# Key transposes moved, layer norm in pairs by twos, constants' loads spaced, the last two experts by output block

## The chip, the cores and the metric

The kernel runs on one core of a Trainium2 chip. The metric is the device time of one execution in microseconds (us); every time below is in us unless it is marked otherwise. TensorE is called PE, VectorE DVE, ScalarE ACT, GpSimd POOL, and SyncE, which here only issues transfers, SP.

## The reference

Two transformer blocks in a row on a sequence of 256 tokens of width 1024. The first block ends in a layer of product keys over 16384 experts, which is where most of the time goes:

```python
scores = jnp.einsum("bshpd,hpnd->bshpn", q, sub_keys)          # 8 heads, 2 halves, 128 keys
s_top, i_top = lax.top_k(scores, 16)                           # per half
best, pos = lax.top_k(cand, 16)                                # cand: sums of the two halves' best
idx = jnp.take_along_axis(cand_idx, pos, axis=-1)
gates = jax.nn.softmax(best, axis=-1)
act = jax.nn.gelu(einsum("td,ted->te", xt, expert_u[idx]), approximate=False)
y = einsum("te,ted->td", gates * act, expert_v[idx])
...
a, b, g = jnp.split(h @ w_in, 3, axis=-1)                      # second block, layer 0
y = conv(a * jax.nn.sigmoid(b)) + db                           # 31 taps
y = jax.nn.silu(layernorm(y, ln_g, ln_b)) * jax.nn.silu(g)
x = x + gt * (y @ w_out)
...                                                            # layer 1: window means
```

Here `gt` and its companions come from a modulation `silu(c) @ w_mod + b_mod` that does not depend on x.

## The kernel before, in words

**Experts without a gather.** The kernel computes all 16384 experts for all 256 tokens and multiplies by a matrix of gates that is zero where an expert was not chosen. `peer_up` multiplies 128 tiles of `expert_u` (128 experts x 1024 each) with the tokens and applies the gelu, `gates` makes the gates and multiplies them on, `peer_down` multiplies with 128 tiles of `expert_v`. Each is done in two halves of 64 tiles. The transposed sum is held in four PSUM tiles `y`.

**Split precision.** Every weight tile is loaded in f32 (`raw`, on SP's queue, three loads ahead). ACT rounds it to `hi`, a subtraction makes `lo` = raw - hi, and PE does three matmuls for each of the 8 blocks of a tile: `hi` with the high part of x (L153), `hi` with its low part (L154), `lo` with the high part (L155). That is 24 matmuls a tile. `hi` and `lo` have three buffers, so ACT can make `hi` of tile n only when PE is through with tile n-3. The subtraction stands on POOL for three of four tiles in the first half of `peer_up`, and on DVE for every fourth (tiles 3, 7, 11, ...) and for all tiles later on (`split_next`, L142).

**Work beside the matmuls.** DVE finds the best keys while the first 64 tiles run. The generator `side` runs `topk` and then `modulation`; `tick` moves it on by one `yield` after every half tile. `topk` works for two blocks of 128 tokens, tb = 0 and 1. For each it does the two searches (MAX, MAX_INDEX, MATCH_REPLACE), then turns positions into keys with a one-hot product: `oh` is a compare with `iota` (L1154), a product (L1156) and three folding sums (L1159, L1160) that leave `sel`, once for each half of the keys. Three PE transposes `ptk` (L1164 to L1166) bring both halves of `sel` and the gates' numerators `exk` into the layout of `gates`; four DVE copies follow (L1167 to L1170). All of it is put into the engines' queues in the order in which it is emitted, modified by a scheduler; each engine runs its queue in order. `behind` ties each step of `topk` to the last subtraction that stands on DVE.

**Into the second block.** `second_prep`, advanced by the same ticks during the second half of `peer_down`, loads constants (`rcnt`, `fwd`, `ftap`, `dw`, `inv`). After the last expert, h is brought up to date with `y`, the sums of squares s2 (`s` in rows) and `acc` (`ssacc` in rows) are made, and `second` begins, with small matmuls of constants (`wfm`, `wfp`) filling PE.

**The layer norm** lies between the gates of the second block (`gate_evac`, four pairs of weight tiles) and its output product, a `quad` of four tiles that goes through the 8 blocks of x two at a time. With `yc` the centred convolution, `dms` the remaining mean and `rl` the inverse deviation, it makes yc\*rl, subtracts dms\*rl, takes Silu with gain and bias, multiplies with Silu of the gate `sg` and splits the product into `xbh` and `xbl`, which PE needs. This goes on four pairs p of blocks; the subtraction of pairs 1 to 3 stands on POOL.

Of the kernel before, what the change touches and what calls it, by code (L numbers as in the profile page):

```python
# [6 lines left out]
F32 = mybir.dt.float32  # L7
# [7 lines left out]
T = 256  # L15
# [25 lines left out]
class Net:  # L41
# [105 lines left out]
    def block(self, ps, x, first=True):  # L147

        hi, lo = self.take()
        xh, xl = x  # L150
        for k in range(KB):
            w = slice(k * 128, (k + 1) * 128)
            self.P.matmul(ps, lhsT=hi[:, w], rhs=xh[:, k, :], start=(k == 0 and first), stop=False, skip_group_check=True)  # L153
            self.P.matmul(ps, lhsT=hi[:, w], rhs=xl[:, k, :], start=False, stop=False, skip_group_check=True)  # L154
            self.P.matmul(ps, lhsT=lo[:, w], rhs=xh[:, k, :], start=False, stop=(k == KB - 1), skip_group_check=True)  # L155
            if k == KB // 2 - 1:
                self.tick()
# [908 lines left out]
    def topk(self):  # L1066
# [12 lines left out]
        for tb in range(2):  # L1079
# [30 lines left out]
            for h in range(8):  # L1110
                V.max(bv[:, h, 0:8], c[:, h, :])
                V.max_index(bi[:, h, 0:8], bv[:, h, 0:8], c[:, h, :])
                t = top.tile([128, 112], F32, tag="mt", bufs=2, name="ct")
                V.match_replace(t, bv[:, h, 0:8], c[:, h, :], LOW)
                V.max(bv[:, h, 8:16], t)
                V.max_index(bi[:, h, 8:16], bv[:, h, 8:16], t)
                yield
                if h % 2 == 0:
                    yield
# [111 lines left out]
    def peer_down(self, act, half):  # L1231
# [53 lines left out]
    def second_prep(self):  # L1285
# [62 lines left out]
    def second(self):  # L1348
# [7 lines left out]

        acc = self.newacc(post)
        s2 = self.psX.tile([128, 512], F32, tag="x", name="s2")[:, 0:T]
        for p in range(4):
            hp = h[:, 2 * p:2 * p + 2, :]  # L1360
            V.tensor_add(hp, self.y[p], hp)
            sq = post.tile([128, 2, T], F32, tag="ta", bufs=2, name="sq2")
            A.activation(sq, hp, AF.Square)
            for i in range(2):
                k = 2 * p + i
                P.matmul(s2, lhsT=self.gf2[:, k, :], rhs=sq[:, i, :], start=(k == 0), stop=(k == KB - 1))
            if p == 0:
                acc = sq
                sq0 = sq
            elif p == 1:  # L1370
                acc = self.newacc(post)
                V.tensor_add(acc, sq0, sq)
            else:
                V.tensor_add(acc, acc, sq)

# [39 lines left out]
        def b_evac(ps, g):  # L1415
# [74 lines left out]
        def ln_gen(po):  # L1490
# [17 lines left out]
            V.tensor_sub(v, v, dm2)  # L1508
# [17 lines left out]
        xb = self.newx(self.cst, "xb")  # L1526
        first = None
        for p in range(4):
            o, sg = (x[:, 2 * p:2 * p + 2, :] for x in (yc, self.sg))
            with self.tc.issue_after(first.ins) if first else nullcontext():  # L1530
                V.tensor_mul(o, o, self.rowb(self.rl))
            i = (G if p else V).tensor_sub(o, o, self.rowb(self.rlm))
            first = first or i
            with self.tc.issue_after(self.lexp.ins):
                A.activation(sg, sg, AF.Silu)
            for i in range(2):
                k = 2 * p + i
                last = A.activation(o[:, i, :], o[:, i, :], AF.Silu, scale=self.col("ln_g", k), bias=self.col("ln_b", k))
# [231 lines left out]
```

## Time and profile before

| | before |
|---|---|
| median of 3 runs (lowest to highest) | 1368.26 (1366.46 to 1369.71) |
| the profiled run, its own time | 1368.67 |
| span of the profiled run | 1366.6 |
| mean granted clock of PE | 0.979 |
| PE busy | 1297.6 (95%) |
| DVE, ACT, POOL busy | 1016.6 (74%), 643.9 (47%), 188.1 (14%) |
| chain that ended last | PE 83%, DVE 10%, ACT 3%, DMA 2% |

The span runs from the first instruction to the last; 2.07 us of the run lie around it. An engine is busy while it has an instruction in work. The chain is followed back from the last instruction to whatever released each step. The granted clock of PE is a share of full speed: 1.00 is 2.4 GHz, 0.50 is 1.2 GHz. A row such as "PE mm L155 <- DVE lo L142" names the instruction that waited and the one that released it.

### The profile page before, as it was taken

To read this page: it belongs to the slowest core of one execution; us is meant where nothing else is said; L and a number is where in the kernel's file an instruction comes from. 1 tells how busy PE (TensorE), PEld (TensorE's weight loads), DVE (VectorE), ACT (ScalarE), POOL (GpSimd) and SP (SyncE) were. 2 spreads that over 40 slices of the span, in tenths; PEclk is the share of its full clock that TensorE was granted. 3 is DMA by queue.
4 is the path that set the end of the run, shared out by engine and by line. 5 is a ranking of instruction groups with operands and counts; after the bars stand their busy time and mean duration, and the time that the engine had idled before them with its cause. 6 is when DMAs were issued, how large, how long until landed. Compare 5 with 4: busy or idle time off the path is not lost.

```text
span 1366.6 us, 27270 instructions
## 1 busy us (share of the span) xinstructions
PE 1297.6 (95%) x11212; PEld 1268.9 (93%) x11212; DVE 1016.6 (74%) x1879; ACT 643.9 (47%) x843; POOL 188.1 (14%) x182
## 2 busy tenths in 40 slices
PE   7999979999988989999999999998999998996988
PEld 7999969989988989999999999997999996996987
DVE  7897765456789865988887999985666656666884
ACT  6675335546443534344445444444444445355662
POOL 0000000003654654000000000010000000001000
PEclk9999999999999999999999999999999998998999
DMA  7644224344654556766666666666777762442553
GB/s 236 206 139 124 93 78 154 124 154 125 187 168 132 178 164 216 230 208 197 216 206 218 213 204 206 212 213 201 237 235 232 234 197 84 126 130 87 170 165 113
DMA packets 67340, 239.69 MB, mean 175 GB/s; under 512 B 8146, under 2 KB 8402, under 8 KB 67088
## 3 DMA queue, kind: packets, MB, share of 16 engines
q1 hardware_dynamic: 59536, 212.79, 51.0%
q0 software_dynamic: 7680, 25.17, 5.4%
q8 instruction: 87, 1.43, 0.4%
q14 instruction: 37, 0.30, 0.1%
HBM read 236.88 MB, written 1.05 MB: 174 GB/s over the span
## 4 chain that ended last, share of the span: by engine, by line
PE 83%; DVE 10%; ACT 3%; DMA 2%; issue 2%; POOL 1%; SPq 0%; DVEq 0%; ACTq 0%; POOLq 0%
PE mm L155 12%; PE mm L153 12%; PE mm L154 12%; PE y L1255 9%; PE y L1257 9%; PE y L1256 9%; DVE lo L142 2%; PE mmv L209 2%; PE mmv L210 2%; PE mmv L211 2%; PE mm L184 2%; PE mm L185 2%; PE mm L183 2%; ACT hi L140 1%; PE G L1210 1%
## 5 line engine op out<-in xcount | busy, mean ns | idle before, releaser
L140 ACT ACTIVATE hi<-raw 128x1024 fp32r<-128x1024 f32 x391 | 412.8, 1060 | 585.4 <-PE mm L154 234.9
L142 DVE TENSOR_TENSOR lo<-raw,hi 128x1024 fp32r<-128x1024 f32 x343 | 420.2, 1228 | 191.6 <-ACT hi L140 189.0
L155 PE MATMUL mm<-xbh,lo 128*128 128x256 f32 x1128 | 319.9, 284 | 5.8 <-DVE lo L142 5.2
L153 PE MATMUL mm<-xbh,hi 128*128 128x256 f32 x1128 | 322.1, 286 | 0.3 <-ACT hi L140 0.3
L154 PE MATMUL mm<-xbl,hi 128*128 128x256 f32 x1128 | 319.0, 283 | 0.0
L1255 PE MATMUL y<-xbh,hi 128*128 128x256 f32 x1024 | 289.5, 283 | 5.2 <-ACT hi L140 5.2
L1257 PE MATMUL y<-xbh,lo 128*128 128x256 f32 x1024 | 288.6, 282 | 0.5 <-DVE lo L142 0.5
L1256 PE MATMUL y<-xbl,hi 128*128 128x256 f32 x1024 | 288.6, 282 | 0.0
L155 PEld LDWEIGHTS mm<-xbh,lo 128*128 128x128 f32 x1128 | 215.0, 191 | 6.8 <-DVE lo L142 6.2
L153 PEld LDWEIGHTS mm<-xbh,hi 128*128 128x128 f32 x1128 | 215.4, 191 | 0.6 <-ACT hi L140 0.5
L154 PEld LDWEIGHTS mm<-xbl,hi 128*128 128x128 f32 x1128 | 215.6, 191 | 0.0
L1255 PEld LDWEIGHTS y<-xbh,hi 128*128 128x128 f32 x1024 | 194.0, 190 | 5.4 <-ACT hi L140 5.4
L1257 PEld LDWEIGHTS y<-xbh,lo 128*128 128x128 f32 x1024 | 193.6, 189 | 1.5 <-DVE lo L142 0.8
L1256 PEld LDWEIGHTS y<-xbl,hi 128*128 128x128 f32 x1024 | 194.1, 190 | 0.0
L142 POOL TENSOR_TENSOR lo<-raw,hi 128x1024 fp32r<-128x1024 f32 x48 | 120.7, 2521 | 200.1 <-ACT hi L140 198.8
L153 PE MATMUL mm<-xah,hi 128*128 128x256 f32 x448 | 128.6, 288 | 3.2 <-ACT xah L1339 3.2
L154 PE MATMUL mm<-xal,hi 128*128 128x256 f32 x448 | 128.0, 286 | 1.0 <-DVE xal L1340 1.0
L155 PE MATMUL mm<-xah,lo 128*128 128x256 f32 x448 | 128.0, 286 | 0.5 <-DVE lo L142 0.5
L1277 POOL DMA_DIRECT2D wm<-in_w_mod x96 | 51.8, 539 | 519.7 <-DVE wm L1280 500.4
L1280 DVE SCALAR_TENSOR_TENSOR wm<-wm,silu_c 128x512 f32<-128x512 f32 x96 | 70.7, 737 | 25.7 <-DMA wm<-in_w_mod 25.3
L153 PEld LDWEIGHTS mm<-xah,hi 128*128 128x128 f32 x448 | 84.9, 190 | 4.5 <-ACT xah L1339 3.4
L154 PEld LDWEIGHTS mm<-xal,hi 128*128 128x128 f32 x448 | 85.0, 190 | 2.1 <-DVE xal L1340 1.2
(456 smaller groups left out, 2191.4 us busy)
## 6 DMA issues: line engine op xcount, KB each, us to landing
raw<-in_U SPq DMA_DIRECT2D x128, 512.0 KB, 3.7
raw<-in_V SPq DMA_DIRECT2D x128, 512.0 KB, 4.1
wm<-in_w_mod POOLq DMA_DIRECT2D x96, 256.0 KB, 3.9
raw<-in_w_in SPq DMA_DIRECT2D x28, 512.0 KB, 3.7
raw<-in_cv_ab SPq DMA_DIRECT2D x16, 512.0 KB, 3.7
raw<-in_pl_in SPq DMA_DIRECT2D x16, 512.0 KB, 4.3
raw<-in_w_xk SPq DMA_DIRECT2D x8, 512.0 KB, 4.7
raw<-in_w_xv SPq DMA_DIRECT2D x8, 512.0 KB, 4.2
```

Source lines behind the costliest of these rows:

```text
L140: self.A.activation(hi, raw, AF.Copy)
L142: i = (self.G if self.order[m][1] else self.V).tensor_sub(lo, raw, hi.bitcast(F32))
L153: self.P.matmul(ps, lhsT=hi[:, w], rhs=xh[:, k, :], start=(k == 0 and first), stop=False, skip_group_check=True)
L154: self.P.matmul(ps, lhsT=hi[:, w], rhs=xl[:, k, :], start=False, stop=False, skip_group_check=True)
L155: self.P.matmul(ps, lhsT=lo[:, w], rhs=xh[:, k, :], start=False, stop=(k == KB - 1), skip_group_check=True)
L183: self.P.matmul(o, lhsT=hi[:, c], rhs=xh[:, k, :], start=a, stop=False, skip_group_check=True)
L184: self.P.matmul(o, lhsT=hi[:, c], rhs=xl[:, k, :], start=False, stop=False, skip_group_check=True)
L1255: P.matmul(o, lhsT=hi[:, w], rhs=wh[:, s, :], start=(j == 0 and db % 2 == 0), stop=False, skip_group_check=True)
L1256: P.matmul(o, lhsT=hi[:, w], rhs=wl[:, s, :], start=False, stop=False, skip_group_check=True)
L1257: P.matmul(o, lhsT=lo[:, w], rhs=wh[:, s, :], start=False, stop=(j == 127), skip_group_check=True)
L1277: nc.gpsimd.dma_start(w, self.I["w_mod"][n, :, 512 * c:512 * (c + 1)])
L1280: V.scalar_tensor_tensor(w, w, 1.0, s, op0=OP.mult, op1=OP.mult, accum_out=part[:, n, c:c + 1])
```

## The change

It has four parts.

1. **Top-k.** The searches pause after every fourth head and no longer after every second, the steps of `oh` pause twice, and six further pauses stand ahead of the transposes. The three transposes are tied to `last_mm`, the last matmul of the tile that PE has in hand when they are emitted.
2. **Layer norm.** `dms` is subtracted from yc before `rl` is known, on DVE for all four pairs. The Silu of the gates is taken straight from PSUM for pairs 0, 1 and 3. The pairs then go in twos: products with `rl` for pairs 0 and 1 first, and that of pair p + 2 only after the split of pair p (`ln_out`). The natural-log table is loaded later, the Silu table once more.
3. **Constants' loads.** `second_prep` pauses 8 half tiles between them.
4. **The last two experts.** `last_pair` goes through them by output block, and `first_out` brings h up to date, squares it and sums it into s2 after each two blocks.

```diff
@@ topk
                     yield
-                    if h % 2 == 0:
+                    if h % 4 == 0:
                         yield
...
                 V.tensor_tensor(oh, abf[:, p].unsqueeze(1).to_broadcast(s4), iota_a, op=OP.is_equal)
-                yield
+                yield from self.pause(2)
                 V.tensor_mul(oh, oh, sif[:, p].unsqueeze(2).to_broadcast(s4))
-                yield
+                yield from self.pause(2)
                 for n in (8, 4, 2):
                     V.tensor_add(oh[:, 0:n], oh[:, 0:n], oh[:, n:2 * n])
                 V.tensor_add(sel[:, p, :].rearrange("q (k h) -> q k h", h=8), oh[:, 0], oh[:, 1])
-                yield
+                yield from self.pause(2)
+            yield from self.pause(6)
...
-            P.transpose(pt[:, 0:128], sel[:, 0, :], self.ident)
-            P.transpose(pt[:, 128:256], sel[:, 1, :], self.ident)
-            P.transpose(pt[:, 256:384], exk.rearrange("q k h -> q (k h)"), self.ident)
+            with self.tc.issue_after(self.last_mm.ins):
+                P.transpose(pt[:, 0:128], sel[:, 0, :], self.ident)
+                P.transpose(pt[:, 128:256], sel[:, 1, :], self.ident)
+                P.transpose(pt[:, 256:384], exk.rearrange("q k h -> q (k h)"), self.ident)
@@ peer_down
             if p < 31:
                 self.spawn(ready(p + 1), True)
+            elif half:
+                self.last_pair(64 + 2 * p)
+                return
...
+    def last_pair(self, j):
...
+        tiles = [self.take(at) for _ in range(2)]
+        for db in range(8):
+            o = self.y[db // 2][:, db % 2, :]
+            w = slice(db * 128, (db + 1) * 128)
+            for i, (hi, lo) in enumerate(tiles):
+                s = (j + i) % 8
+                P.matmul(o, lhsT=hi[:, w], rhs=wh[:, s, :], start=False, stop=False, skip_group_check=True)
...
+            if db % 2:
+                self.first_out(db // 2)
+                self.tick()
...
+    def first_out(self, p):
...
+        V.tensor_add(hp, self.y[p], hp)
+        sq = post.tile([128, 2, T], F32, tag="sq2", bufs=2, name="sq2")
+        A.activation(sq, hp, AF.Square)
+        for i in range(2):
+            k = 2 * p + i
+            P.matmul(self.s2, lhsT=self.gf2[:, k, :], rhs=sq[:, i, :], start=(k == 0), stop=(k == KB - 1))
@@ second_prep
         nc.sync.dma_start(self.rcnt, I["rcnt"])
+        yield from self.pause(8)
         f = pool.tile([128, 2, 4, 128], F32, tag="rawc", name="fwd")
         nc.sync.dma_start(f, I["fwd"])
+        yield from self.pause(8)
@@ second, ln_gen and after
-            A.activation(dms, dm, AF.Copy, scale=1.0 / D)
+            self.ln_exp(A.activation(dms, dm, AF.Copy, scale=1.0 / D))
...
+            with self.tc.issue_after(self.lexp.ins):
+                A.preload_act_table(AF.Silu)
+            with self.tc.issue_after(i.ins):
+                for p in range(4):
+                    o = yc[:, 2 * p:2 * p + 2, :]
+                    V.tensor_sub(o, o, self.rowb(dms))
...
+            with self.tc.issue_after(split[p - 2].ins) if p > 1 else nullcontext():
                 V.tensor_mul(o, o, self.rowb(self.rl))
-            i = (G if p else V).tensor_sub(o, o, self.rowb(self.rlm))
...
             V.tensor_mul(o, o, sg)
-            self.splitx(o, xb, slice(2 * p, 2 * p + 2), True)
+            x = [t[:, 2 * p:2 * p + 2, :] for t in xb]
+            V.tensor_copy(x[0], o)
+            split.append(V.tensor_sub(x[1], o, x[0].bitcast(F32)))
```

What this does to the engines' queues follows at three places, in the program's order. The first is **PE, at the first transposes (tb = 0)**. Before, one transpose stands inside tile 24, after one matmul of it:

```order
L155 MATMUL mm<-xbh,lo 128x256
L153 MATMUL mm<-xbh,hi 128x256
L1164 MATMUL ptk<-ident,sel 128x128
L154 MATMUL mm<-xbl,hi 128x256
L155 MATMUL mm<-xbh,lo 128x256
```

and the other two follow 41 matmuls later, inside tile 25. With the change all three stand in a row:

```order
L154 MATMUL mm<-xbl,hi 128x256
L155 MATMUL mm<-xbh,lo 128x256
L1167 MATMUL ptk<-ident,sel 128x128
L1168 MATMUL ptk<-ident,sel 128x128
L1169 MATMUL ptk<-ident,exk 128x128
L153 MATMUL mm<-xbh,hi 128x256
```

The first transpose has moved 71 instructions down PE's queue, to the boundary between tiles 26 and 27. For tb = 1 the same three moved from tiles 48 (its start) and 49 to the boundary between tiles 53 and 54.

The second place is **DVE, in the search for tb = 0, from the first `sel` on**. Before, `lo` of tile 23 stands ten rows ahead of the first row shown, and the `lo` at the end is that of tile 27:

```order
L1160 TENSOR_TENSOR sel<-oh 128x128
L1154 TENSOR_TENSOR oh<-abf,iota_3604 128x2048
L1156 TENSOR_TENSOR oh<-oh,sif 128x2048
L1159 TENSOR_TENSOR oh<-oh 128x1024
L1159 TENSOR_TENSOR oh<-oh 128x512
L1159 TENSOR_TENSOR oh<-oh 128x256
L1160 TENSOR_TENSOR sel<-oh 128x128
L142 TENSOR_TENSOR lo<-raw,hi 128x1024
```

With the change, where the two `lo` are those of tiles 23 and 27:

```order
L1161 TENSOR_TENSOR sel<-oh 128x128
L1155 TENSOR_TENSOR oh<-abf,iota_3604 128x2048
L142 TENSOR_TENSOR lo<-raw,hi 128x1024
L1157 TENSOR_TENSOR oh<-oh,sif 128x2048
L1160 TENSOR_TENSOR oh<-oh 128x1024
L1160 TENSOR_TENSOR oh<-oh 128x512
L1160 TENSOR_TENSOR oh<-oh 128x256
L1161 TENSOR_TENSOR sel<-oh 128x128
L142 TENSOR_TENSOR lo<-raw,hi 128x1024
```

The whole first product, its sums and the second compare now stand ahead of `lo` of tile 23, and only the second product and sums between that one and the next. Behind the last `lo` shown, 10 search instructions fewer than before stand ahead of `lo` of tile 31. For tb = 1 the first product, its sums and the second compare and product stand between `lo` of tiles 47 and 51, and the second sums between 51 and 55; before, all of it stood between 47 and 51.

The third place is **ACT in the layer norm**, from `dms` to the last Silu of yc. Before:

```order
L1503 ACTIVATE dms<-dm 128x256
L1505 ACTIVATE dm_14847<-dm 128x256
L140 ACTIVATE hi<-raw 128x1024
L1510 ACTIVATE rl<-lv 128x256
L1517 ACTIVATE sg<-mm 128x512
L1511 ACTIVATE rl<-rl 128x256
L1535 ACT_TABLE_LOAD
L1535 ACTIVATE sg<-sg 128x512 x3
L140 ACTIVATE hi<-raw 128x1024 x2
L1517 ACTIVATE sg<-mm 128x512
L1538 ACTIVATE yc<-yc,cols 128x256 x2
L1535 ACTIVATE sg<-sg 128x512
```

After:

```order
L312 ACT_TABLE_LOAD
L1531 ACTIVATE dm_14846<-dm 128x256
L1536 ACTIVATE rl<-lv 128x256
L140 ACTIVATE hi<-raw 128x1024
L1548 ACTIVATE sg<-mm 128x512
L1537 ACTIVATE rl<-rl 128x256
L1539 ACT_TABLE_LOAD
L140 ACTIVATE hi<-raw 128x1024 x2
L1548 ACTIVATE sg<-mm 128x512
L1565 ACTIVATE yc<-yc,cols 128x256 x6
L1568 ACTIVATE sg<-sg 128x512
L1565 ACTIVATE yc<-yc,cols 128x256 x2
```

The three Silu of `sg` behind the table load are gone, and the Silu of yc follow at once on `sg` of pair 3. One table load more, for Silu, stands ahead of `sg` of pair 0, and the natural-log load stands between `dms` and `dm` (it was earlier). On DVE the rows from `lv` on now are four subtractions of `dms`, then products of `rl` for two pairs, then product with `sg`, `xbh` and `xbl` pair by pair; POOL has none of it.

Two things the queues show not to have moved. On SP the loads of `rcnt`, `fwd`, `ftap` and `dw` stand in a row in both, with the same two loads of `expert_v` behind them and then `inv`, and the same waits. On PE, behind the last `y` matmul, both have one `wfm`, four `s`, four `wfp`, four `s`, and then before two `wfp` and the two matmuls of `cs`, and now `wfp`, the two of `cs`, `wfp`. The loads of the modulation's input (`silu_c`) and what hangs on it stand six tiles later.

## Rows read from the trace of the kernel before

**Rows 1.** Waits of TensorE over the whole run: total, times, longest, in us.

```profile
PE ptk L1164 <- DVE sel L1160: 10.8, 2, 5.4
...
PE mm L155 <- DVE lo L142: 6.7, 6, 4.4
...
PE y L1255 <- ACT hi L140: 5.2, 1, 5.2
```

**Rows 2.** Table by stretch: length, five engines' busy us (instructions), granted clock, DMA, GB/s.

```profile
401.70:408.60 6.90, 3.71 (x18) 3.71 (x19) 6.73 (x14) 0.00 (x0) 1.99 (x1) 0.51 0.51 154
...
429.00:435.90 6.90, 4.43 (x21) 4.44 (x22) 6.87 (x36) 0.00 (x0) 1.33 (x1) 0.51 0.50 165
...
487.00:490.60 3.60, 3.40 (x17) 3.40 (x18) 3.46 (x5) 0.00 (x0) 0.00 (x0) 0.53 0.73 218
...
1157.50:1162.00 4.50, 2.91 (x25) 2.72 (x24) 3.48 (x4) 3.40 (x5) 0.00 (x0) 1.00 0.61 211
...
1250.80:1255.00 4.20, 3.52 (x15) 3.23 (x16) 4.17 (x9) 0.74 (x1) 0.00 (x0) 0.50 0.02 10
...
1303.50:1309.70 6.20, 2.96 (x14) 2.91 (x14) 6.20 (x13) 3.17 (x6) 0.00 (x0) 0.72 0.66 200
```

**Rows 3.** Timeline of DVE in the top-k stage: start, duration, instruction, idle time before.

```profile
369.08 1.23 DVE L142 TENSOR_TENSOR lo<-raw,hi 128x1024 fp32r<-128x1024 f32 x1
...
380.48 1.23 DVE L142 TENSOR_TENSOR lo<-raw,hi 128x1024 fp32r<-128x1024 f32 x1 [4.47 <-ACT hi L140]
...
394.15 1.24 DVE L142 TENSOR_TENSOR lo<-raw,hi 128x1024 fp32r<-128x1024 f32 x1
...
395.29 3.43 DVE L1156 TENSOR_TENSOR oh<-oh,sif 128x2048 f16<-128x2048 f16 x1
...
406.13 1.22 DVE L1156 TENSOR_TENSOR oh<-oh,sif 128x2048 f16<-128x2048 f16 x1
...
407.38 1.48 DVE L1159 TENSOR_TENSOR oh<-oh 128x1024 f16<-128x1024 f16 x3
...
476.64 1.25 DVE L142 TENSOR_TENSOR lo<-raw,hi 128x1024 fp32r<-128x1024 f32 x1
...
486.86 0.29 DVE L1160 TENSOR_TENSOR sel<-oh 128x128 f32<-128x128 f16 x1
```

**Rows 4.** Timeline of POOL in the same stage.

```profile
389.07 2.40 POOL L142 TENSOR_TENSOR lo<-raw,hi 128x1024 fp32r<-128x1024 f32 x1 [0.45 <-ACT hi L140]
...
394.76 8.93 POOL L142 TENSOR_TENSOR lo<-raw,hi 128x1024 fp32r<-128x1024 f32 x3 [3.29 <-ACT hi L140]
```

**Rows 5.** Timeline of the layer norm: ACT, then DVE, POOL and PE.

```profile
1237.14 1.28 ACT L1535 ACT_TABLE_LOAD   x1
...
1238.43 1.68 ACT L1535 ACTIVATE sg<-sg 128x512 f32<-128x512 f32 x3
...
1240.01 1.99 ACT L140 ACTIVATE hi<-raw 128x1024 fp32r<-128x1024 f32 x2
...
1242.95 1.09 ACT L1538 ACTIVATE yc<-yc,cols 128x256 f32<-128x256 f32 x2 [0.47 <-DVE yc L1532]
...
1252.66 0.41 DVE L284 CAST xbh<-yc 128x512 fp32r<-128x512 f32 x1
...
1253.00 0.68 DVE L1539 TENSOR_TENSOR yc<-yc,sg 128x512 f32<-128x512 f32 x1
...
1243.66 5.45 POOL L1532 TENSOR_TENSOR yc<-yc,dms 128x512 f32<-128x512 f32 x3 [24.13 <-DVE yc L1531]
...
1250.74 0.77 PE L183 MATMUL mm<-xbh,hi 128*128 128x256 f32 x2 [10.10 <-DVE xbh L284]
...
1252.19 0.58 PE L184 MATMUL mm<-xbl,hi 128*128 128x256 f32 x1 [0.68 <-DVE xbl L287]
```

**Rows 6.** Timeline of DVE after the last `y` matmul.

```profile
1138.65 0.42 DVE L1378 TENSOR_SCALAR v<-s 128x256 f32<-128x256 f32 x1 [4.48 <-PE s L1366]
```

**Rows 7.** Timeline of ACT where the second half of `peer_down` begins.

```profile
936.74 1.06 ACT L140 ACTIVATE hi<-raw 128x1024 fp32r<-128x1024 f32 x1 [9.30 <-DMA raw<-in_V]
```

More of the change, by code (lines that the diff above doesn't have):

```diff
@@ L154, in block @@
             self.P.matmul(ps, lhsT=hi[:, w], rhs=xl[:, k, :], start=False, stop=False, skip_group_check=True)
-            self.P.matmul(ps, lhsT=lo[:, w], rhs=xh[:, k, :], start=False, stop=(k == KB - 1), skip_group_check=True)
+            self.last_mm = self.P.matmul(ps, lhsT=lo[:, w], rhs=xh[:, k, :], start=False, stop=(k == KB - 1),
+                                         skip_group_check=True)
             if k == KB // 2 - 1:
@@ L1117, in topk @@
                 yield
-                if h % 2 == 0:
+                if h % 4 == 0:
                     yield
@@ L1258, in peer_down @@
                 self.tick()
+    def last_pair(self, j):
+        P = self.P
+        wh, wl = self.ring
+        at = self.pos
+        tiles = [self.take(at) for _ in range(2)]
[5 more added lines that the diff above has]
+                P.matmul(o, lhsT=hi[:, w], rhs=wh[:, s, :], start=False, stop=False, skip_group_check=True)
+                P.matmul(o, lhsT=hi[:, w], rhs=wl[:, s, :], start=False, stop=False, skip_group_check=True)
+                P.matmul(o, lhsT=lo[:, w], rhs=wh[:, s, :], start=False, stop=(i == 1), skip_group_check=True)
+            if db % 2:
+                self.first_out(db // 2)
+                self.tick()
+    def first_out(self, p):
+        post, V, A, P = self.post1, self.V, self.A, self.P
+        if p == 0:
+            self.s2 = self.psX.tile([128, 512], F32, tag="x", name="s2")[:, 0:T]
+        hp = self.h[:, 2 * p:2 * p + 2, :]
+        V.tensor_add(hp, self.y[p], hp)
[4 more added lines that the diff above has]
+            P.matmul(self.s2, lhsT=self.gf2[:, k, :], rhs=sq[:, i, :], start=(k == 0), stop=(k == KB - 1))
+        if p == 0:
+            self.sq0 = sq
+        elif p == 1:
+            self.acc2 = post.tile([128, 2, T], F32, tag="rawc", name="acc2")
+            V.tensor_add(self.acc2, self.sq0, sq)
+        else:
+            V.tensor_add(self.acc2, self.acc2, sq)
     def modulation(self):
@@ L1315, in second_prep @@
         nc.sync.dma_start(inv, I["inv"])
-        yield
-        yield
+        yield from self.pause(8)
         self.ih = pool.tile([128, 3, T], F32R, name="ih")
@@ L1355, in second @@
         self.st2 = post
[L1357 to L1374, printed above, removed]
+        acc, s2 = self.acc2, self.s2
         v2 = post.tile([128, T], F32, name="v2")
@@ L1507, in ln_gen @@
             V.tensor_scalar(v, dsq, 1.0 / D, EPS, op0=OP.mult, op1=OP.add)
[L1508 removed]
+            i = V.tensor_sub(v, v, dm2)
             r = self.rl = post.tile([128, T], F32, name="rl")
@@ L1511, in ln_gen @@
             self.lexp = A.activation(r, r, AF.Exp, scale=-0.5)
+            with self.tc.issue_after(self.lexp.ins):
[4 more added lines that the diff above has]
+                    V.tensor_sub(o, o, self.rowb(dms))
             self.rsqrt2(post, v, r)
-            V.tensor_mul(dms, dms, r)
-            self.rlm = dms
         def gate_evac(ps, p):
-            A.activation(self.sg[:, 2 * p:2 * p + 2, :], ps, AF.Copy)
+            with self.tc.issue_after(self.lexp.ins) if p == 3 else nullcontext():
+                A.activation(self.sg[:, 2 * p:2 * p + 2, :], ps, AF.Copy if p == 2 else AF.Silu)
             yield
@@ L1526, in second, with ln_out @@
         xb = self.newx(self.cst, "xb")
-        first = None
-        for p in range(4):
+        def ln_out(p):
             o, sg = (x[:, 2 * p:2 * p + 2, :] for x in (yc, self.sg))
-            with self.tc.issue_after(first.ins) if first else nullcontext():
+            with self.tc.issue_after(split[p - 2].ins) if p > 1 else nullcontext():
                 V.tensor_mul(o, o, self.rowb(self.rl))
-            i = (G if p else V).tensor_sub(o, o, self.rowb(self.rlm))
-            first = first or i
-            with self.tc.issue_after(self.lexp.ins):
-                A.activation(sg, sg, AF.Silu)
             for i in range(2):
                 k = 2 * p + i
-                last = A.activation(o[:, i, :], o[:, i, :], AF.Silu, scale=self.col("ln_g", k), bias=self.col("ln_b", k))
-            V.tensor_mul(o, o, sg)
-            self.splitx(o, xb, slice(2 * p, 2 * p + 2), True)
+                self.lsilu = A.activation(o[:, i, :], o[:, i, :], AF.Silu, scale=self.col("ln_g", k), bias=self.col("ln_b", k))
+            if p == 2:
+                with self.tc.issue_after(self.lsilu.ins):
+                    self.lsilu = A.activation(sg, sg, AF.Silu)
+            yield
+            V.tensor_mul(o, o, sg)
+            x = [t[:, 2 * p:2 * p + 2, :] for t in xb]
+            V.tensor_copy(x[0], o)
+            split.append(V.tensor_sub(x[1], o, x[0].bitcast(F32)))
+            yield
+        split = []
+        lo = [ln_out(p) for p in range(4)]
+        next(lo[0])
+        next(lo[1])
+        for p in range(4):
+            next(lo[p])
+            if p < 2:
+                next(lo[p + 2])
+        last = self.lsilu
         self.ln_exp(last)
```

4 lines of the change are left out of this document (1 added, 3 removed).

## Prediction

> **What bounds the kernel now.** I read the table of engines first: PE is busy 95% of the span and makes up 83% of the chain that ended last, so time is gained only where PE stands idle or runs at half clock. The next view is therefore the list of what PE waited for. Its longest entries are `ptk`, which waited twice for `sel`, 10.8 us in all, and `xbh` of the layer norm, one wait of 10.10 us [rows 1, 5]. The largest of the six waits for `lo`, 4.4 us, falls into the same top-k stage, and the wait of `y` for `hi`, 5.2 us, into the start of the second half of `peer_down` [rows 1]. The change touches all four places. The table by stretch then shows what each wait leaves behind: after the three of the top-k stage PE works at a granted clock of 0.51 to 0.53, its lower level of 1.2 GHz, for 3.71, 4.43 and 3.40 us of busy time, and after the layer norm at 0.50 for 3.52 us [rows 2]. An idle time of 1.59 us (4.50 less 2.91 busy) left the clock at 1.00; one of 3.24 us (6.20 less 2.96) brought the mean to 0.72 [rows 2].
>
> **Top-k: what is removed.** Both waits for `sel` are gone if `sel` is ready by the new places. With the `lo` wait that goes with them that is 10.8 + 4.4 = 15.2 us. Half clock costs a little under half of the busy time in it, 11.5 us in sum, so about 5.2, or 1.75 for each drop. Together 20.4 us.
>
> **Top-k: what comes.** DVE is the engine that was late, and its work is the same; only its order against `lo` changes, so I look for `lo` waits. Four tiles take 11.4 us (`lo` at 369.08 and 380.48) [rows 3]. `hi` of a tile starts when PE leaves the tile three before; `lo` is wanted two tiles and two matmuls later, 5.9 us, less 1.0 for `hi` and 1.2 for `lo`: a `lo` may start 3.6 us late without a wait. The one at 394.15 came 13.67 after its forerunner, so 2.3 late, and PE did not wait.
> DVE is slowed by POOL. The same product takes 3.43 us while POOL makes its `lo` and 1.22 once POOL is idle [rows 3, 4]. From 476.64 to 487.15 DVE had `lo`, product, sums and `sel`, which alone take 1.2 + 1.15 + 1.1 + 0.3 = 3.7 us; it took 10.5 beside three POOL subtractions, so each costs 2.3 us where only such operations stand in line [rows 3].
> - `lo` of tile 23: ahead of it are now a `lo`, compare, product, sums, `sel`, a second compare and some small ones, 7.0 us alone; the stretch is long enough for four POOL subtractions, 9.2. That is 16.2, 4.8 more than 11.4. With `lo` of tile 19 up to 1.8 late, the wait is 1.2 to 3.0 us; I take 1.9.
> - `lo` of tile 27: 3.7 alone and three times 2.3 are 10.6, less than 11.4. `sel` is then ready ahead of the transposes, which stand at the same tile. No wait.
> - `lo` of tile 31: the first gates, and 10 searches fewer. About 7.8 alone, 5.5 of it slowed; with three to four POOL subtractions 14.7 to 17, so 0 to 2.9 us of wait. Searches don't slow down beside POOL, and `lo` of tile 27 comes in time, so I take 0.
> - `lo` of tile 51: `lo` of tile 47 starts 2.3 late as its like at 394.15 does; then the 10.5 us above, compare and product 2.3, one POOL subtraction more 2.3. That is 15.1, 3.7 too long; 2.3 + 3.7 - 3.6 = 2.4 us of wait. The bounds are 0 (POOL idle meanwhile) and 3.8. The transposes behind it have what they need: sums and `sel`, 1.4 alone and at most two POOL subtractions, end within the three tiles (8.5 us) that lie between.
> In sum 4.3 us, between 1.2 and 9.7. Whether waits of 2 us drop the clock no row decides: between 1.59 and 3.24 I take one of two halves, 0.9. **Gain 20.4 - 4.3 - 0.9 = 15.2 us**; at the worst 20.4 - 9.7 - 3 x 1.75 = 5.5, at the best 19.2.
>
> **Layer norm.** PE left the gates at 1240.64, restarted at 1250.74, and its second matmul, which wants `xbl`, came at 1252.19 [rows 5]. The three POOL subtractions, 5.45 us, leave the path, and so do three Silu of the gates, 1.68 [rows 5]. The new path begins at the same place, since the last `hi` waits for PE to leave the gates: `hi` 1.0, `sg` of pair 3 0.6, two Silu of yc 1.09, product with `sg` 0.65, `xbh` 0.35 give 1244.3 for the first matmul; the second pair's Silu and product, then `xbl` 0.65, give 1245.8 for the second [rows 5]. Four subtractions now stand ahead of a `lo` of the gates' last tile, so I add 0.4. That is 1246.2 against 1252.19, **a gain of 6.0 us**. The rest follows: a cut of the `quad` is 24 matmuls, 2.85 us, and pairs 1 to 3 come every 1.6 to 2.8 us. If the clock stays up, 1.3 more is gained; if ACT is 2 us late, 4.0 is left. I take 6.0 and bounds of 4.0 and 7.5.
> The table loads cost nothing here by the rows: the load took 1.28 us and the next ACTIVATE began at once, 0.01 later [rows 5], and the added one on this path has `hi` of the last tile to hide behind, with about 0.6 to spare. The Trainium skill (ScalarE: Activation LUTs, What ACT_TABLE_LOAD costs) counts 2.66 us for a switch, a drain of 1.38 behind the load. By that rule the layer norm would gain an estimated 5.2; the row shows no such drain.
>
> **The last two experts.** PE's queue behind the last `y` matmul is the same but for one exchange of `wfp` and `cs`. PE was busy from there without a gap, and DVE stood 4.48 us for the last `s` [rows 6]. The first two squares come earlier, but nothing waited for them alone. Cost 0, between a gain of 0.7 (ACT's chain behind `cs`, one `wfp` earlier) and a loss of 0.7 (the square roots now ahead of `xah` on ACT).
>
> **Constants' loads.** SP's queue is the same, row for row. ACT waited 9.30 us for an `expert_v` tile queued behind four constants [rows 7]; it will again. 0. The shift of the modulation by six tiles, 17 us, hides behind the rest of `peer_down`; if that cover failed, the first `lo` behind it on DVE would wait.
>
> **Sum.** 15.2 + 6.0 = 21.2 us off the profiled run's 1368.67, whose median of three is 1368.26: 1347.
>
> **The rivals.**
> - *The `lo` waits take the place.* POOL's three `lo` lie densely (8.93 us for three, 2.98 each against 2.40 alone) [rows 4]; if every one stops DVE for 2.4 us, tiles 23, 31 and 51 wait near their upper bounds and the clock falls three times. The stage gains 5.5 and the whole 9.5 to 11.5: 1357 to 1359. For it speaks that DVE was at work all through those stretches (6.73 of 6.90 us, 6.87 of 6.90) [rows 2]; against it that DVE has the searches, which run on. The Trainium skill (SBUF — State Buffer, SBUF: two separate sides) says that a DVE operation with two SBUF inputs and a POOL operation exclude each other for the whole instruction. By that rule this rival is the one to fear; the trace agrees in kind (3.43 against 1.22).
> - *Slower.* The same mechanism on the other side: if a POOL subtraction holds DVE for 2.98 us, the whole of its share of 8.93, then tiles 19, 23, 27, 31, 47 and 51 wait 28 us together and six drops cost 10.5. 38.5 less 20.4 is a loss of 18, less 6 for the layer norm: 1380. It decides from about 2.75 us a subtraction; 2.3 was measured.
> - *The constants do spread.* If their loads went out apart, the `y` wait of 5.2 us and some 2.7 of half clock behind it would go too: 1339. Against it stands the unchanged queue.
> - *Nothing measurable.* The first rival at its worst, with ACT late in the layer norm as well: about 1366.
>
> **How the numbers follow.** 0.62 for the sum, whose own range is 1343 to 1351; 0.22 for the first rival, 0.05 for the slower one, 0.08 for the constants, 0.03 for nothing. The range 1341 to 1358 leaves out the constants, the slower case, nothing, and a corner of the first rival, under 2 in 10. Faster by over 0.2% (2.7 us, about what a measurement of this kernel can tell from no change) are the forecast, the first rival and the constants: 0.92; within it 0.03; slower 0.05.
>
> **What would show it.** In the changed profile `ptk` should be gone from PE's waits, `lo` should stand there with 1 to 3 us at two places of the top-k stage, near tiles 23 and 51, and the stretches at half clock there should fall from three to one or none. The wait for `xbh` should be 4 us, with no POOL beside it. The wait of `y` for `hi` should still be some 5 us. I am wrong if `ptk` waits on, if three or more `lo` waits exceed 3 us, or if the wait of `y` is gone.

## The result and the profile after

The median fell from 1367.36 (1365.77 to 1369.71, 4 runs) to 1357.28 (1356.61 to 1357.57, 4 runs): a ratio of 0.9924, 95% interval 0.9907 to 0.9941. That is faster by 10 us; forecast were 21. The time lies inside the forecast range of 1341 to 1358, 0.7 us from its slow end.

| | before | after |
|---|---|---|
| profiled run, its own time | 1368.67 | 1357.57 |
| span | 1366.6 | 1355.0 |
| mean granted clock | 0.979 | 0.983 |
| PE, DVE, ACT, POOL busy | 1297.6, 1016.6, 643.9, 188.1 | 1295.6, 1013.2, 643.0, 182.4 |
| first `y` matmul starts (end of the top-k stage and the gates) | 736.92 | 730.37 |
| first filler `wfm`, behind the last `y` | 1128.58 | 1121.04 |
| first `mmv` of the second block | 1143.64 | 1138.52 |
| second matmul of the `quad` behind the layer norm | 1252.19 | 1240.91 |

The last four lines are starts of the same PE instruction in both traces. Their differences cut the 11.6 us of span into places: top-k 6.55, the rest up to the fillers 1.0, the fillers **minus 2.4** (15.07 before, 17.47 after), from `mmv` to the `quad` 6.2, the rest 0.3. "Fillers" stands here and below for the stretch from the first `wfm` to the first `mmv`.

Waits of PE after (total, times, longest); `ptk` is gone, and `lo` has doubled against [rows 1]:

```profile
PE mm L155 <- DVE lo L142: 13.7, 9, 4.9
...
PE y L1261 <- ACT hi L140: 3.8, 1, 3.8
...
PE mm L184 <- DVE xbh L1572: 3.8, 1, 3.8
```

Timeline of PE after: start, duration, instruction, idle time before it and its releaser.

```profile
375.22 0.39 PE L155 MATMUL mm<-xbh,lo 128*128 128x256 f32 x1 [1.54 <-DVE lo L142]
...
404.34 0.58 PE L155 MATMUL mm<-xbh,lo 128*128 128x256 f32 x1 [4.82 <-DVE lo L142]
...
490.39 0.58 PE L155 MATMUL mm<-xbh,lo 128*128 128x256 f32 x1 [4.86 <-DVE lo L142]
...
1121.04 1.12 PE L1420 MATMUL wfm<-dw,ftap 31*128 31x512 f32 x2
...
1138.52 0.58 PE L210 MATMUL mmv<-hi,xah 128*128 128x256 f32 x1 [1.84 <-ACT xah L1384]
...
1239.80 0.47 PE L184 MATMUL mm<-xbh,hi 128*128 128x256 f32 x2 [3.77 <-DVE xbh L1572]
...
1240.91 0.45 PE L185 MATMUL mm<-xbl,hi 128*128 128x256 f32 x1 [0.64 <-DVE xbl L1573]
```

Three waits for `lo`, at tiles 15, 23 and 51, are 11.2 us, where the ones they replace were 15.2. The table by stretch (columns as in [rows 2]) shows two stretches at half clock in the top-k stage instead of three, and in its last two rows a third place, among the fillers, where the clock falls although PE is busy throughout:

```profile
401.40:408.30 6.90, 3.96 (x18) 3.96 (x19) 5.72 (x6) 0.00 (x0) 1.80 (x1) 0.51 0.44 129
...
490.10:493.60 3.50, 3.21 (x15) 3.21 (x16) 1.85 (x5) 0.00 (x0) 0.00 (x0) 0.51 0.62 179
...
1125.50:1128.40 2.90, 2.90 (x10) 1.33 (x9) 0.07 (x1) 2.07 (x4) 0.00 (x0) 1.00 0.63 226
...
1128.50:1130.00 1.50, 1.50 (x5) 1.19 (x4) 0.00 (x0) 0.00 (x0) 0.00 (x0) 0.50 0.00 0
```

The clock fell in this place before as well, but for a shorter time. The whole stretch of fillers, before and then after, had a mean clock of 0.85 and 0.71:

```profile
1128.50:1143.60 15.10, 13.28 (x36) 6.91 (x34) 7.76 (x14) 8.99 (x18) 0.00 (x0) 0.85 0.25 72
...
1121.00:1138.50 17.50, 15.68 (x35) 7.27 (x34) 7.48 (x14) 9.83 (x19) 0.00 (x0) 0.71 0.19 62
```

Timelines of DVE and POOL after, for [rows 3, 4] and the layer norm:

```profile
372.08 3.09 DVE L142 TENSOR_TENSOR lo<-raw,hi 128x1024 fp32r<-128x1024 f32 x1
...
385.35 1.26 DVE L142 TENSOR_TENSOR lo<-raw,hi 128x1024 fp32r<-128x1024 f32 x1
...
397.54 3.46 DVE L1155 TENSOR_TENSOR oh<-abf,iota 128x2048 f16<-128x2048 f16 x1
...
400.93 3.36 DVE L142 TENSOR_TENSOR lo<-raw,hi 128x1024 fp32r<-128x1024 f32 x1
...
471.80 1.22 DVE L142 TENSOR_TENSOR lo<-raw,hi 128x1024 fp32r<-128x1024 f32 x1
...
483.66 3.40 DVE L1157 TENSOR_TENSOR oh<-oh,sif 128x2048 f16<-128x2048 f16 x1
...
486.98 3.36 DVE L142 TENSOR_TENSOR lo<-raw,hi 128x1024 fp32r<-128x1024 f32 x1
...
1229.88 2.49 DVE L1543 TENSOR_TENSOR yc<-yc,dms 128x512 f32<-128x512 f32 x4
```

```profile
371.70 2.39 POOL L142 TENSOR_TENSOR lo<-raw,hi 128x1024 fp32r<-128x1024 f32 x1 [3.33 <-ACT hi L140]
...
400.46 2.74 POOL L142 TENSOR_TENSOR lo<-raw,hi 128x1024 fp32r<-128x1024 f32 x1 [0.54 <-ACT hi L140]
...
472.33 9.10 POOL L142 TENSOR_TENSOR lo<-raw,hi 128x1024 fp32r<-128x1024 f32 x3 [3.23 <-ACT hi L140]
...
486.41 2.85 POOL L142 TENSOR_TENSOR lo<-raw,hi 128x1024 fp32r<-128x1024 f32 x1 [0.43 <-ACT hi L140]
```

Each of the three late `lo` (372.08, 400.93, 486.98) took 3.1 to 3.4 us, and every other one of DVE in this stage 1.2 to 1.3. POOL had begun a `lo` of its own 0.4 to 0.6 us ahead of each of the three, at 371.70, 400.46 and 486.41. Where DVE began first it was not held: its `lo` at 471.80 took 1.22, with POOL's beginning at 472.33. Timeline of ACT after, for [rows 5, 7]:

```profile
928.89 1.06 ACT L140 ACTIVATE hi<-raw 128x1024 fp32r<-128x1024 f32 x1 [8.37 <-DMA raw<-in_V]
...
1232.21 1.28 ACT L1539 ACT_TABLE_LOAD   x1
...
1233.51 1.06 ACT L140 ACTIVATE hi<-raw 128x1024 fp32r<-128x1024 f32 x1
```

The `quad` waited 3.77 us where it had waited 10.10, no POOL work stands beside it, and ACT waited 8.37 us for the tile behind the constants, as it had 9.30.

### The profile page after: what moved, and what is told of

It reads as the page before. It is cut to its first block, busy times and chain, and to the rows that moved or that the text cites. A ratio compares the mean times of both kernels' runs of the same rounds, so it can differ in the third digit from the quotient of the medians.

```text
span 1355.0 us, 27261 instructions
## 1 busy us (share of the span) xinstructions
PE 1295.6 (96%) x11212; PEld 1264.5 (93%) x11212; DVE 1013.2 (75%) x1881; ACT 643.0 (47%) x841; POOL 182.4 (13%) x179
## 4 chain that ended last, share of the span: by engine, by line
PE 84%; DVE 9%; ACT 2%; DMA 2%; issue 2%; SPq 0%; DVEq 0%; ACTq 0%
PE mm L155 12%; PE mm L153 12%; PE mm L154 12%; PE y L1261 9%; PE y L1263 9%; PE y L1262 9%; DVE lo L142 3%; PE mm L185 2%; PE mm L186 2%; PE mm L184 2%; PE mmv L210 1%; PE mmv L212 1%; PE mmv L211 1%; PE G L1213 1%; ACT hi L140 1%
## 5 line engine op out<-in xcount | busy, mean ns | idle before, releaser
L142 DVE TENSOR_TENSOR lo<-raw,hi 128x1024 fp32r<-128x1024 f32 x343 | 424.6, 1241 | 182.4 <-ACT hi L140 181.5
L1261 PE MATMUL y<-xbh,hi 128*128 128x256 f32 x1008 | 285.3, 284 | 3.8 <-ACT hi L140 3.8
L1262 PE MATMUL y<-xbl,hi 128*128 128x256 f32 x1008 | 284.5, 283 | 0.0
L1263 PE MATMUL y<-xbh,lo 128*128 128x256 f32 x1008 | 283.8, 282 | 0.8 <-DVE lo L142 0.8
L1261 PEld LDWEIGHTS y<-xbh,hi 128*128 128x128 f32 x1008 | 191.1, 190 | 4.0 <-ACT hi L140 4.0
L1263 PEld LDWEIGHTS y<-xbh,lo 128*128 128x128 f32 x1008 | 190.6, 189 | 1.7 <-DVE lo L142 1.0
L1262 PEld LDWEIGHTS y<-xbl,hi 128*128 128x128 f32 x1008 | 191.3, 190 | 0.0
L155 PEld LDWEIGHTS mm<-xah,lo 128*128 128x128 f32 x448 | 85.1, 190 | 1.8 <-issue 1.0
```

What stands on the lines that cost most here:

```text
L142: i = (self.G if self.order[m][1] else self.V).tensor_sub(lo, raw, hi.bitcast(F32))
L155: self.last_mm = self.P.matmul(ps, lhsT=lo[:, w], rhs=xh[:, k, :], start=False, stop=(k == KB - 1), skip_group_check=True)
L1261: P.matmul(o, lhsT=hi[:, w], rhs=wh[:, s, :], start=(j == 0 and db % 2 == 0), stop=False, skip_group_check=True)
L1262: P.matmul(o, lhsT=hi[:, w], rhs=wl[:, s, :], start=False, stop=False, skip_group_check=True)
L1263: P.matmul(o, lhsT=lo[:, w], rhs=wh[:, s, :], start=False, stop=(j == 127), skip_group_check=True)
```

## The experiments

Each part was first run alone on the kernel before. Times are medians of 10 runs there and of 4 or 5 in the later experiments; a ratio is to the kernel before, run beside it, with its 95% interval.

**Top-k part alone:** of the change only the hunks on `last_mm` and `topk`.

```diff
-                if h % 2 == 0:
+                if h % 4 == 0:
 ...
+            yield from self.pause(6)
 ...
+            with self.tc.issue_after(self.last_mm.ins):
+                P.transpose(pt[:, 0:128], sel[:, 0, :], self.ident)
```

> The kernel before with the top-k part alone. Theory (the parts add up; lo of tiles 23 and 51 is late and then runs beside a POOL subtraction itself): two lo waits of 4.8 us near tiles 23 and 51, one of 1.5 near tile 15, ptk gone from the waits; 6 to 7 us less than before. Rival (the shift of the modulation or the other parts cost the rest): the full 15 us, with lo waits of 2 us. The wait of y for hi should fall from 5.2 to about 3.8 us if this part brought that too.

1360.88, ratio 0.9947 (0.9928 to 0.9966): 7 us by the ratio, 8 by the medians. The first `y` came at 728.49, 8.4 earlier. Its timeline of PE and a stretch of its table:

```profile
404.76 0.58 PE L155 MATMUL mm<-xbh,lo 128*128 128x256 f32 x1 [4.87 <-DVE lo L142]
...
489.59 0.39 PE L155 MATMUL mm<-xbh,lo 128*128 128x256 f32 x1 [2.48 <-DVE lo L142]
```

```profile
489.60:493.00 3.40, 3.40 (x28) 3.40 (x29) 3.33 (x3) 0.00 (x0) 2.18 (x1) 1.00 0.71 211
```

The part alone gives about half of the 15.2. The waits stand where they stand in the whole change, with one difference: at tile 51 it was 2.48 us, and the clock stayed up behind it.

**Layer norm alone:** only the hunks of `second` from `zh` on.

```diff
-            i = (G if p else V).tensor_sub(o, o, self.rowb(self.rlm))
 ...
+                for p in range(4):
+                    o = yc[:, 2 * p:2 * p + 2, :]
+                    V.tensor_sub(o, o, self.rowb(dms))
```

> The kernel before with the layer norm alone. Theory: the wait for xbh falls from 10.1 to 3.8 us, 6 us less than before, nothing else moves. Rival (the gain after the change came partly from what arrived earlier upstream): 3 to 4 us less.

1363.01, ratio 0.9968 (0.9949 to 0.9986): 4.4 us by the ratio, 6.0 by the medians (1368.99 before), and in its trace 6.6 from `mmv` to the second matmul of the `quad` (101.95 against 108.55). PE's wait there:

```profile
1244.51 0.68 PE L183 MATMUL mm<-xbh,hi 128*128 128x256 f32 x2 [3.77 <-DVE xbh L1544]
```

**Last pair alone:** only `last_pair`, `first_out` and the lines that they replace.

```diff
+            elif half:
+                self.last_pair(64 + 2 * p)
+                return
 ...
+        acc, s2 = self.acc2, self.s2
```

> The kernel before with the last pair by output block alone. Theory (its exchange of wfp and cs puts xah behind a wf on ACT, and the clock then falls ahead of them): 2 to 3 us more than before, half clock from about 7 us after the last y matmul to the first mmv. Rival (the loss after the change came from another phase of the clock, moved by what changed upstream): within 1 us of before, with half clock as before.

1369.51, ratio 1.0012 (0.9995 to 1.0028): no difference measured. From the first filler to `mmv` it took 13.59 us, with no half clock, and not the 17.47 of the whole change. That the new order by itself costs the 2.4 us is not supported.

**Constants' pauses alone:** only the hunks of `second_prep`.

```diff
         nc.sync.dma_start(self.rcnt, I["rcnt"])
+        yield from self.pause(8)
```

> The kernel before with the pauses between the constants' loads alone. Theory (the queues are the same): within 0.2% of before, and a y wait of 5.2 us. Rival (the pauses spread the loads, the y wait falls to 3.8 us): 1 to 2 us less.

1368.65, ratio 1.0004 (0.9983 to 1.0025): no difference measured. Its timelines of SP's queue and of PE show why: the first and the last of the four constants' loads are still issued within 1.8 us, and `y` waits on.

```profile
917.92 0.33 SPq L1292 DMA_DIRECT2D rcnt<-in_rcnt  x1
...
919.43 0.26 SPq L1300 DMA_DIRECT2D dw<-in_cv_dw  x1
```

```profile
936.66 0.58 PE L1255 MATMUL y<-xbh,hi 128*128 128x256 f32 x1 [4.63 <-ACT hi L140]
```

By the ratios the four parts together give 0.53 + 0.32 - 0.12 - 0.04 = 0.69%, 9.4 us, and the whole change gave 0.76%: it is nearly the sum of its parts, and most of what is missing from the forecast is already missing in the top-k part alone.

**The change without its last pair:** the loop over p goes to its end, and `second` makes `acc` and `s2` as before.

```diff
-            elif half:
-                self.last_pair(64 + 2 * p)
-                return
```

> The changed kernel with the last pair undone. Theory (this part costs time by its order behind the last y): 2 to 3 us less than the changed kernel, about 1354.8. Rival (a phase of the clock): 1357, with half clock from 7 us after the last y on as in the changed kernel.

1352.98, ratio 0.988 (0.9852 to 0.9908), filler to `mmv` 13.42. Taken alone this would convict the last pair, but its top-k stage also differs, with no code changed there: `lo` waited 2.50 us at tile 23 without a fall of the clock, and the first `y` came 3.5 earlier than in the first run of the change. So the **change itself ran once more**, unaltered:

> The changed kernel once more, unaltered. Theory (where the clock falls in the stretch of fillers is not set by the order of instructions): the stretch from the first filler to the first mmv differs by 1.5 us or more from the 17.5 us of the first profile, and the length of the lo waits near tiles 23 and 51 may differ too. Rival (the order sets it): 17.5 us again within 0.5.

1356.72, ratio 0.9914 (0.9897 to 0.9931). Its timelines of PE and DVE, and its stretch behind tile 51:

```profile
487.20 0.39 PE L155 MATMUL mm<-xbh,lo 128*128 128x256 f32 x1 [2.49 <-DVE lo L142]
...
1121.06 1.12 PE L1420 MATMUL wfm<-dw,ftap 31*128 31x512 f32 x2
...
1134.65 0.58 PE L210 MATMUL mmv<-hi,xah 128*128 128x256 f32 x1 [1.84 <-ACT xah L1384]
```

```profile
482.61 1.23 DVE L1157 TENSOR_TENSOR oh<-oh,sif 128x2048 f16<-128x2048 f16 x1
...
483.75 3.39 DVE L142 TENSOR_TENSOR lo<-raw,hi 128x1024 fp32r<-128x1024 f32 x1
```

```profile
487.20:491.00 3.80, 3.80 (x21) 3.80 (x22) 3.70 (x4) 0.00 (x0) 2.19 (x1) 0.61 0.76 237
```

The same instructions from first filler to `mmv` took 13.59 us here and 17.47 in the first run. And at tile 51 the product passed at 1.23 us, POOL then caught `lo` alone (3.39), and the wait was 2.49 and not 4.86. Both vary from run to run of one kernel. The profiled runs of this kernel and of the one without the last pair, 1354.49 and 1354.16, are alike in this stretch (13.59 and 13.42), though 3.7 us lie between their medians.

**`lo` of tiles 23 and 51 on POOL** (on the change).

```diff
-        add([I["U"][b] for b in range(64)], "GGGV")
+        add([I["U"][b] for b in range(64)], "".join("G" if b in (23, 51) else "GGGV"[b % 4] for b in range(64)))
```

> The changed kernel with lo of tiles 23 and 51 on POOL in place of DVE, so that no subtraction stands behind the one-hot work on DVE. Theory (DVE's late lo, itself slowed by POOL, is the wait): the two waits of 4.8 us and both half-clock stretches go; 9 to 12 us less than the changed kernel if POOL keeps up, since seven POOL subtractions in a row take 17 to 21 us and seven tiles 20. Rival (POOL is the bound there): as many us of waits, now for POOL's lo.

1352.09, ratio 0.9871 (0.9842 to 0.9899): some 5 us less than the change, and not the 9 to 12 expected. Both long `lo` waits are gone; with more POOL work beside it `sel` was late once, and there the clock fell:

```profile
413.93 0.48 PE L1168 MATMUL ptk<-ident,sel 128*128 128x128 f32 x1 [4.03 <-DVE sel L1161]
```

**A longer pause behind the first `sel`,** so that the second compare no longer stands ahead of `lo` of tile 23. In the first of two kernels the final pause gives it back (6 to 2) and the transposes keep their place; in the second, called e8, it does not, and the transposes come two and four tiles later than in the change.

```diff
-                yield from self.pause(2)
+                yield from self.pause(2 if p else 6)
 ...
-            yield from self.pause(6)
+            yield from self.pause(2)
```

> The changed kernel with four pauses more between the two one-hot selections and four fewer behind them: the second compare, and for tb = 1 its product too, stand behind lo of tiles 23 and 51, the transposes where they were. Theory (3.4 us of compare beside POOL ahead of lo): the lo wait near tile 23 falls from 4.8 to 1.5 or less, that near tile 51 likewise; the transposes may now wait up to 3 us for sel. 4 to 8 us less than the changed kernel. Rival (the wait is set by POOL's lo alone): the same 4.8 us waits.

1350.62, ratio 0.9868 (0.9844 to 0.9892). At tile 23 nothing waits any more; the longest waits are now at tile 31 and at tile 47 (473.95), and shorter. The clock fell at both all the same, to a mean of 0.50 from 424.20 to 428.00 and of 0.57 from 474.00 to 478.00:

```profile
424.15 0.58 PE L155 MATMUL mm<-xbh,lo 128*128 128x256 f32 x1 [2.80 <-DVE lo L142]
...
473.95 0.39 PE L155 MATMUL mm<-xbh,lo 128*128 128x256 f32 x1 [1.79 <-DVE lo L142]
```

The second kernel, e8, has the first of the two edits only.

> As the run before it, but without taking pauses from behind: the transposes two tiles (tb = 0) and four tiles (tb = 1) later. Theory: the lo waits fall as there and the transposes don't wait; 6 to 9 us less than the changed kernel. Rival (the gates made later crowd lo of tile 31): a new lo wait of 2 to 4 us there.

1346.93 (1345.08 to 1353.66), ratio 0.9855 (0.9818 to 0.9893): some 10 us less than the change. No wait of the top-k stage is above 1.6 us, and none is followed by half clock. Its longest wait, and DVE around tile 23:

```profile
435.91 0.39 PE L155 MATMUL mm<-xbh,lo 128*128 128x256 f32 x1 [1.58 <-DVE lo L142]
```

```profile
397.86 1.22 DVE L142 TENSOR_TENSOR lo<-raw,hi 128x1024 fp32r<-128x1024 f32 x1
...
399.00 3.43 DVE L1155 TENSOR_TENSOR oh<-abf,iota 128x2048 f16<-128x2048 f16 x1
...
409.61 1.22 DVE L142 TENSOR_TENSOR lo<-raw,hi 128x1024 fp32r<-128x1024 f32 x1
```

`lo` comes ahead of the compare and takes 1.22; the compare behind it takes 3.43 instead, where PE does not wait for it. The first `y` starts at 719.82, 17.1 earlier than before. But here too the clock fell among the fillers, 6 us into them with PE fully busy, and they took 18.83:

```profile
1113.00:1115.40 2.40, 2.40 (x7) 1.06 (x6) 2.40 (x4) 2.40 (x6) 0.00 (x0) 1.00 0.25 20
...
1115.40:1120.00 4.60, 4.60 (x10) 2.56 (x9) 1.21 (x2) 1.54 (x3) 0.00 (x0) 0.50 0.55 217
```

**e8 without the last pair,** with the three lines of `peer_down` taken out as above.

> The selections apart as in e8, with the last pair undone. Theory by now (the last pair itself costs nothing; how long the stretch of fillers runs at half clock decides): the stretch lasts 13.4 us without and 15 to 19 us with half clock, and the time is within 4 us of e8, to either side. Rival (the last pair costs by its order): 2 to 5 us less than e8.

1346.99, ratio 0.985 (0.9827 to 0.9873): no difference from the one with it. The fillers took 17.74 with half clock, so the long stretch comes without the last pair as well.

**The square sums ahead of the constants' matmuls** (e8, and in addition `wfp` tied behind the last `s`; called e9).

```diff
-            P.matmul(self.s2, lhsT=self.gf2[:, k, :], rhs=sq[:, i, :], start=(k == 0), stop=(k == KB - 1))
+            self.last_s2 = P.matmul(self.s2, lhsT=self.gf2[:, k, :], rhs=sq[:, i, :], start=(k == 0), stop=(k == KB - 1))
 ...
-                P.matmul(ps, lhsT=self.ftap[:, m, :], rhs=self.dw[:, c * 512:(c + 1) * 512], start=True, stop=True)
+                with self.tc.issue_after(self.last_s2.ins) if m else nullcontext():
+                    P.matmul(ps, lhsT=self.ftap[:, m, :], rhs=self.dw[:, c * 512:(c + 1) * 512], start=True, stop=True)
```

> The selections apart and the transposes later (as in the run e8), and in addition the wfp matmuls tied behind the last s matmul, so that PE sums the squares as soon as they are there. Theory (the four wfp, 3.7 to 4.5 us, that stand between the second and the third pair of s hide what the last pair by output block could give): from the first filler to the first mmv 9 to 11 us instead of 13.4 to 18.8; 4 to 7 us less than e8. Rival (ACT's and DVE's chain behind the sum is the bound): within 1 us of e8.

1343.24, ratio 0.9814 (0.979 to 0.9838), the fastest of all. The expectation for the stretch was missed all the same; timelines of PE and ACT:

```profile
1112.66 1.12 PE L1421 MATMUL wfm<-dw,ftap 31*128 31x512 f32 x2
...
1118.52 3.69 PE L1421 MATMUL wfp<-dw,ftap 31*128 31x512 f32 x8
...
1122.14 2.08 PE L266 MATMUL cs<-acc,ones 128*128 128x256 f32 x4
...
1124.15 3.78 PE L1421 MATMUL wfp<-dw,ftap 31*128 31x512 f32 x4
...
1127.86 0.58 PE L210 MATMUL mmv<-hi,xah 128*128 128x256 f32 x1
```

```profile
1122.74 0.89 ACT L1384 ACTIVATE xah<-mi,mod 128x256 fp32r<-128x256 f32 x2
```

`xah` was begun 10.1 us after the first filler, but `mmv` came 15.2 after it, without a wait: the last fillers, `cs` and `wfp`, stood ahead of it in PE's queue, at half clock.

**e9 without the last pair,** as above; `wfp` is tied behind the last `s` in its old place.

> As e9, with the last pair undone: wfp behind s, experts tile by tile. Theory (summing inside the last pair has the squares ready 2 to 4 us earlier once PE takes them): 2 to 4 us more than e9. Rival (the order of s and wfp is the whole gain): the same time as e9 within 1 us.

1346.47, ratio 0.9844 (0.9824 to 0.9863); `xah` was begun 11.0 us after the first filler, `mmv` 13.4, with no half clock there. By the medians this is 3.2 us slower than with the last pair. The intervals of the two ratios overlap, but all five runs (1344.65 to 1347.54) are slower than all five with it (1337.80 to 1343.92). The traces don't show the gain in this stretch, which took 1.8 us longer with the last pair.

## Why the prediction was right and where it was wrong

**The number.** The time is inside the range, but the forecast itself, 21 us less, was missed by half: the range was drawn wide enough to take in nearly all of the first rival, and it is there that the time fell. By the prediction's own signs, `ptk` is gone, the wait of `y` stands and that for `xbh` is 3.8 us; the `lo` waits were 4.8 us and not 1 to 3, and two stretches at half clock were left and not one or none.

**The step that failed is "Top-k: what comes", the term of 4.3 us for the `lo` waits;** it measured 11.2. The starts in it were right: `lo` of tile 23 was put 16.2 us behind that of tile 19 and came 15.6 behind it (385.35 and 400.93), and that of tile 51 was put 15.1 behind tile 47's and came 15.2 behind it (471.80 and 486.98). What was wrong is `lo` itself: it was priced at 1.2 us, its time with POOL idle, while the operations ahead of it were charged for POOL. The trace of before had such a `lo` to show, 1.85 us at 429.56 beside one of POOL begun at 427.94. Here it took 3.36, which is 2.1 more at each of the two tiles, out of the 2.9 and 2.5 by which these waits exceed their terms of 1.9 and 2.4. The third, 1.54 at tile 15, has the same cause: that `lo`, which the prediction didn't look at, took 3.09. So 5.8 of the 6.9 us too many are POOL's share of the `lo` that PE waits for; the other 1.1 is not traced further. With the two longer waits the clock came down, 3.96 and 3.21 us of busy time at 0.51, so about 3.5 lost against 0.9. With 11.2 and 3.5 the sum reads 20.4 - 11.2 - 3.5 = 5.7, and the trace has 6.55.

The experiments show that these waits come from a `lo` that stands on DVE behind the one-hot work: where the `lo` of tile 23 is put ahead of the compare, it takes 1.22 and its wait is gone; where tiles 23 and 51 leave DVE, both their waits are gone. Both edits take away the late start and the slow `lo` at once, so the split between them is read from the durations above and not from an experiment; no run took away POOL's work alone. By the start of the first `y`, four traces with the old top-k stage (736.1 to 738.3) have a mean of 736.90, the four with the change's (726.9 to 730.4) 728.28, the four with the selections of e8 (719.8 to 722.5) 721.05. So the change gives 8.6 there on average, and e8's selections 15.8, about the 15.2 that the prediction had for the change.

Tiles 27 and 31 did not make PE wait, as predicted, and neither did the transposes.

**The first rival** has the kind of thing that happened: the `lo` waits took the place, by POOL, and the time is within its 1357 to 1359. Its working is not what happened. It has every POOL subtraction stop DVE for longer, so that `lo` starts later; the starts were as forecast, and `lo` itself was slow. The waits at tiles 23 and 51 went past its bounds of 3.0 and 3.8, tile 15 waited and not tile 31, and the clock fell twice and not three times. That its number fits is partly luck: 2.4 us of it come from the fillers, which no rival had. **The slower rival** asked that every POOL subtraction cost DVE 2.75 us or more; the three late `lo` were held up by 1.9 to 2.1. The Trainium skill (SBUF — State Buffer, SBUF: two separate sides) says that DVE operations with two SBUF inputs and POOL operations that read SBUF exclude each other, and the trace agrees: 3.36 beside POOL's 2.74 at 400.46, 1.22 without. `lo` is such an operation too, and that the sum left out.

**Layer norm: right.** 6.0 predicted, 6.2 in the trace; first matmul at 1239.80 with a wait of 3.77 where 4 was given, the second 1.11 behind it (1.5 was given). The table load at 1232.21 took 1.28, and the next ACTIVATE began 0.02 behind its end; no drain of 1.38 shows.

**Constants: right,** 0. The loads went out together as before, and the `y` wait is 3.8 to 5.2 us in every kernel.

**Last two experts: right by order, with bounds of 0.7 that were too tight for the stretch.** The instructions from the first filler to `mmv` take 13.4 to 18.8 us, and over the 14 traces this goes by how long the clock is at half in them: 13.4 to 13.6 us where it fell not at all or only in the wait for `xah` at the end, 15.1 to 15.3 with 3.4 to 5.8 us of half clock, 17.5 to 18.8 with 10.0 to 12.9. It is not tied to the last pair: 13.6 with it alone, 13.6 and 17.5 for the very same kernel, 17.7 without it. The first run of the change happened to have a long one.

Open stay two things. What decides whether and when the clock falls among the fillers: no kernel here varied that alone. And whether the last pair gains: with the square sums first the kernel was 3 us faster with it, in e8 the same, alone 1.6 us slower by the ratio with an interval that allows no difference, and in the change itself 4 us slower by the medians, with ratios whose intervals just meet.

## What to carry to other kernels

When an operation that PE waits for runs on an engine that another one slows down, charge it the slowed price as well as everything queued ahead of it: here some 2 us forgotten at each of three tiles, with starts right to 0.6 us, became 6 us of waits, and the clock came down at two of them. Then look for an order in which the contention falls on an operation for which nobody waits: the pause that puts `lo` ahead of the compare, with the transposes later, brought the stage's gain from 8.6 to 15.8 us, and the kernel to 1346.93. And before a difference of 2 to 4 us in one stretch is explained by the order in it, run the same kernel a second time.

## What the runs showed of the hardware that was not expected

- The granted clock fell to half while PE was busy without a gap: 1.00 from 1125.50 to 1128.40, then 0.50, among matmuls of constants from 31 rows and of `s` in f32. Identical instructions took 13.59 us in one run and 17.47 in another.
- A wait of 2.5 us ends either way: behind 2.48 the clock stayed at 1.00, behind 2.49 a stretch of 3.80 us had a mean of 0.61, and behind one of only 1.79 (tile 47 with the longer pause) 4.00 us had 0.57.
- How DVE and POOL meet differs from run to run: with the same program the product ahead of tile 51 took 3.40 us in one run and 1.23 in another, and PE's wait was 4.86 or 2.49.
